# Masks first, a bf16 gate product of three exact parts, and the scores of two heads side by side

## Chip, cores and metric

The kernel runs on one core of one Trainium2 chip. The metric is the device time of one execution in microseconds (us), the median of the runs; lower is better.

## The reference

The program has three parts. Block 1 is two layers of a hybrid attention over 256 tokens of width 1024; block 2 is a gated delta-rule scan with a context of 256 rows; behind it stand 16 experts and a final norm. The change lies in block 1 alone. Each of its layers projects the modulated rows to 4032 columns and mixes three kinds of attention with heads of 64:

```python
def dsa_mixer(q, k, v, iq, ik, iw):      # 4 heads, one key head; block of 128 queries
    isc = einsum("bthd,bsd->bths", iqb, ik)
    isc = einsum("bth,bths->bts", iwb, relu(isc))
    _, idx = top_k(where(causal, isc, -inf), topk)      # topk = 64
    p = masked_softmax(einsum(qb, k[idx]) * scale, idx <= tpos)
...
def fox_mixer(q, k, v, logf):            # 6 heads
    cum = cumsum(logf, axis=1)
    s = einsum("bthd,bshd->bhts", qb, k) * scale
    s = s + cum[t] - cum[s]              # forget gates
    p = masked_softmax(s, causal)
...
def nsa_mixer(q, q_rot, kc, vc, ks, vs, kw, vw, gates):   # 6 heads, 2 groups of keys
    s = einsum("btgjd,bcgd->bgjtc", qb, kc) * scale       # 15 compressed keys
    p_cmp = masked_softmax(s, cend <= tpos)
    ...                                   # selected blocks and window: at 256 tokens both plain causal
    o = g0 * o_cmp + g1 * o_slc + g2 * o_win
```

With 256 tokens the selection and the window of the third kind take in everything that is causal, so each is an ordinary causal attention.

## The kernel before

A layer of block 1 (`layer`) goes through 17 chunks of projection columns. Each chunk's weights come by DMA into one of two tiles `w`, are split into two exact halves (`halves`, ScalarE and VectorE or GpSimd) and multiplied on TensorE in three products of one pass each (`proj_t`, L419 to L421; `proj_n`, L443). As soon as a chunk has given the queries and keys of two heads, their attention is called: `dsa` for two pairs, `fox` for three, and `nsa`, which after the compressed branch calls a pair for each of three head pairs and two branches. That makes 2 sparse, 3 gated and 6 plain pairs a layer, 22 in both. Other work is put in by hooks: products of modulation vectors (`gemv`, L358), and parts of the context for block 2. The order of the instructions on each engine is laid down by a scheduler when the program is built, from the dependencies and its own estimates, so that products of several stages stand between one another on TensorE.

`pair` treats two heads at once. Head 0 has rows 0 to 63 of `qT` and `kT`, head 1 rows 64 to 127. The scores of a head fill a half of a PSUM tile `s` [128, 2, 512]: the later block of 128 queries against 256 keys in columns 0 to 255, the earlier block against 128 keys in columns 256 to 383. For each block and head the score opens the sum (L526), the gate product over 12 f32 rows follows in gated pairs (L529), and the mask closes it: a bf16 product of a scaled identity `bigI` with the triangle `trib` (L532) or with the sparse mask of `topk` (L534). Then come the maxima on VectorE (L536, L537), four exponentials on ScalarE (L545), scaling by the reciprocal sums, transposes through a second tile `s` (L572 to L574), copies out of it, and the products with the values (L562, L565). There are two tiles `s`; the indexer's scores (L788) and other transposes use them too.

The gate's operands are prepared behind the first chunk (`after_na`): cumulated log gates from a product, `foxr` by VectorE (L759) and `foxc` by ScalarE (L761); `fox_rows` (GpSimd, L771) makes one head's 12 rows. `nsa` computes the compressed scores by 12 products with 64 rows and 16 columns and 12 masks (L870, L871).

Block 2 and the experts follow. The experts' weights are loaded into tiles `rw` by SP (L1766, L1808), which lie where tiles of block 2 lay and wait for these.

Of the kernel before, what the change touches and what calls it, by code (L numbers as in the profile page):

```python
# [11 lines left out]
BF = mybir.dt.bfloat16  # L12
AF = mybir.ActivationFunctionType
ALU = mybir.AluOpType
AX = mybir.AxisListType
PSUM = bass.MemoryType.PSUM

D = 1024
T = 256
# [9 lines left out]
# the tiles of block 2 from the lowest address up, those first that are needed longest: the weights of the experts  # L29
# take over from above  # L30
# [9 lines left out]
# ---------------------------------------------------------------- layout of the columns  # L40
# [65 lines left out]
# ---------------------------------------------------------------- constants of the shapes  # L106
def _consts():
    p = np.arange(128)
    c = {}
# [34 lines left out]
    # [cum8; -cum8] rows to the two operands of the forget-gate product  # L144
    fx = np.zeros((128, 14))
    for h in range(6):
        fx[h, h] = 1            # a1*hm
        fx[6 + h, 6 + h] = 1    # a0*hm
    fx[6:12, 12] = 1            # b1
    fx[0:6, 13] = 1             # b0  # L150
# [31 lines left out]
def prep(inp):  # L182
    """Layout of the inputs: transposes, slices, permutations of rows and columns."""
    f = {k: np.asarray(v) for k, v in inp.items()}
    a = {}
# [48 lines left out]
class Kern:  # L234
# [12 lines left out]
    def after(self, last):  # L247
        """what follows on the engine of this instruction is issued behind it"""
        return self.tc.issue_after(last.ins) if last is not None else nullcontext()
# [5 lines left out]
    def scope(self, name, psum=True, order=()):  # L255
        """pools for the working tiles of one part of the program"""
# [15 lines left out]
    def side(self):  # L272
        """what blocks 1 and 2 share: parts of the weights, and the rows of the context"""
# [7 lines left out]
    # ---- tiles  # L281
# [39 lines left out]
    # ---- exact halves of an operand: w = hi + lo, both of the type that goes through in one pass  # L321
# [21 lines left out]
    def gemv(self, w_dram, sec, vec, b_row, whole=False):  # L343
        """rows 32j.. of [128, 256]: columns 256j.. of the section of w_dram"""
# [19 lines left out]
    def cols(self, acc, outs):  # L364
        """outs: (i, out [128, 8], add, gain): out = (columns of the vector at row i + add) * gain"""
# [13 lines left out]
    def bcast(self, acc, out, add):  # L379
        """out [128, 1024]: the vector on every partition, plus add"""  # L380
# [25 lines left out]
    # ---- projections  # L406
# [6 lines left out]
    def proj_t(self, out, w, uT):  # L413
        """out [128 columns, 256 t]; w [128, 8, 128]"""
# [1493 lines left out]
```

## Time and profile before

| | |
|---|---|
| median of three runs | 1374.69 us (1373.82 to 1382.97) |
| the profiled execution, span from first to last instruction | 1373.8 us; it lies 0.9 us below the median |
| TensorE matmuls busy | 1122.8 us, 82% |
| VectorE busy | 566.2 us, 41% |
| ScalarE busy | 389.0 us, 28% |
| GpSimd busy | 274.7 us, 20% |
| HBM read | 327.51 MB, 239 GB/s over the span |
| mean granted TensorE clock | 0.872 |

A busy share is a mean over stages that have different limits; what counts is the share in the stage of the change. The duration of a matmul in the trace is that of its way through the array, and one begins before the one ahead has ended; so what an instruction takes from TensorE is read from its start to the next start. An f32 product appears as two instructions (x2).

### The profile page before, as it was taken

The numbers are of one execution on the slowest core, as the hardware profiler recorded it, in microseconds if no ns is written. First come the engines' busy times: TensorE is split into PE (matmuls) and PEld (weight loads), VectorE is DVE, ScalarE is ACT, GpSimd is POOL, SyncE is SP. The second block draws the span as 40 slices with busy tenths as digits, with TensorE's granted clock in tenths as the row PEclk, the third lists the DMA queues.
The fourth block names the chain that finished last, engine by engine and source line by source line (L and its number), as shares of the span: only waits on it lengthen the run. The fifth ranks groups of instructions, "written<-read, shape, count | busy, mean of one in ns | idle before, by whom it ended". The sixth has DMA issues, their size and how long they took to land.

```text
span 1373.8 us, 22174 instructions
## 1 busy us (share of the span) xinstructions
PE 1122.8 (82%) x9158; PEld 788.2 (57%) x9158; DVE 566.2 (41%) x1307; ACT 389.0 (28%) x891; POOL 274.7 (20%) x235
## 2 busy tenths in 40 slices
PE   5889999987879999993988989989766666676665
PEld 2667687676756877672977977765422232232222
DVE  2484235767587233559667545641100010010002
ACT  2242234745333332644444242520000000000001
POOL 1431031156420121125334434200000000000000
PEclk9998988998988798996997999999866787788876
DMA  9745854342415245660212153879999999999996
GB/s 336 266 152 174 308 189 146 102 159 102 161 62 170 92 171 186 233 203 14 93 36 81 62 215 125 340 277 408 411 409 411 410 410 411 408 412 409 411 412 231
DMA packets 93526, 330.01 MB, mean 240 GB/s; under 512 B 8048, under 2 KB 22256, under 8 KB 87024
## 3 DMA queue, kind: packets, MB, share of 16 engines
q1 hardware_dynamic: 93424, 328.58, 63.8%
q8 instruction: 72, 1.18, 0.3%
q14 instruction: 30, 0.25, 0.0%
HBM read 327.51 MB, written 1.05 MB: 239 GB/s over the span
## 4 chain that ended last, share of the span: by engine, by line
DMA 27%; PE 26%; DVE 4%; ACT 3%; issue 3%; POOL 2%; SPq 0%; POOLq 0%; DVEq 0%; ACTq 0%
DMA rw<-in_w_up 13%; DMA rw<-in_w_down 9%; DMA rw<-in_w_gate 5%; PE s L1281 3%; PE s L461 2%; PE mm L419 2%; PE mm L420 2%; PE mm L421 2%; PE g L1770 1%; PE mm L1813 1%; PE s L526 1%; PE mm L443 1%; PE s L1417 1%; PE o L1770 1%; PE g L358 1%
## 5 line engine op out<-in xcount | busy, mean ns | idle before, releaser
L421 PE MATMUL mm<-uT,wl 128*128 128x256 f32 x576 | 168.6, 295 | 17.4 <-DVE wl L331 9.1
L419 PE MATMUL mm<-uT,wh 128*128 128x256 f32 x576 | 173.9, 302 | 9.9 <-DVE yT L1216 6.1
L330 ACT CAST wh<-w 128x1024 fp32r<-128x1024 f32 x124 | 127.7, 1034 | 181.9 <-PE mm L420 112.0
L420 PE MATMUL mm<-uT,wh 128*128 128x256 f32 x576 | 169.0, 294 | 0.0
L331 POOL TENSOR_TENSOR wl<-w,wh 128x1024 fp32r<-128x1024 f32 x47 | 116.1, 2473 | 205.3 <-ACT wh L330 204.1
L421 PEld LDWEIGHTS mm<-uT,wl 128*128 128x128 f32 x576 | 112.8, 197 | 24.6 <-DVE wl L331 10.2
L419 PEld LDWEIGHTS mm<-uT,wh 128*128 128x128 f32 x576 | 113.9, 198 | 21.8 <-issue 8.8
L1770 PE MATMUL g<-rw,XE 128*32 128x256 f32 x928 | 86.9, 483 | 43.0 <-DMA rw<-in_w_up 43.0
L1770 PE MATMUL o<-rw,XE 128*32 128x256 f32 x944 | 89.0, 482 | 36.3 <-DMA rw<-in_w_gate 36.3
L420 PEld LDWEIGHTS mm<-uT,wh 128*128 128x128 f32 x576 | 113.8, 197 | 5.5 <-issue 4.9
L331 DVE TENSOR_TENSOR wl<-w,wh 128x1024 fp32r<-128x1024 f32 x77 | 96.7, 1256 | 46.8 <-ACT wh L330 46.5
L1786 DVE TENSOR_TENSOR hd<-hd,g 128x256 f32<-128x256 f32 x16 | 6.7, 419 | 219.0 <-PE g L1770 219.0
L1782 ACT ACTIVATE hd<-o 128x256 f32<-128x256 f32 x16 | 6.1, 384 | 320.6 <-PE o L1770 320.6
L1770 PEld LDWEIGHTS g<-rw,XE 128*32 128x32 f32 x928 | 32.1, 129 | 90.1 <-DMA rw<-in_w_up 70.7
L1813 PE MATMUL mm<-rw,hT 128*32 128x256 f32 x880 | 64.2, 426 | 23.9 <-DMA rw<-in_w_down 18.3
L1770 PEld LDWEIGHTS o<-rw,XE 128*32 128x32 f32 x944 | 31.8, 129 | 83.5 <-DMA rw<-in_w_gate 59.1
L443 PE MATMUL mm<-wh,uT 128*128 128x256 f32 x256 | 62.2, 330 | 3.2 <-ACT wh L330 2.5
L526 PE MATMUL s<-qk 64*128 64x256 f32 (+1 forms) x176 | 57.2, 408 | 0.3 <-DVE qk L514 0.2
L1813 PEld LDWEIGHTS mm<-rw,hT 128*32 128x32 f32 x880 | 27.3, 119 | 51.9 <-DMA rw<-in_w_down 27.0
L443 PEld LDWEIGHTS mm<-wh,uT 128*128 128x128 f32 x256 | 49.0, 228 | 7.4 <-ACT wh L330 2.9
L545 ACT ACTIVATE P<-s,nm 128x256 f32<-128x256 f32 (+1 forms) x88 | 35.8, 419 | 40.9 <-DVE nm L538 40.9
L443 PE MATMUL mm<-wl,uT 128*128 128x256 f32 x128 | 42.5, 332 | 0.7 <-DVE wl L331 0.7
(640 smaller groups left out, 2116.5 us busy)
## 6 DMA issues: line engine op xcount, KB each, us to landing
rw<-in_w_gate SPq DMA_DIRECT2D x59, 1024.0 KB, 18.4
rw<-in_w_up SPq DMA_DIRECT2D x58, 1024.0 KB, 18.4
rw<-in_w_down SPq DMA_DIRECT2D x55, 1024.0 KB, 18.6
w<-in_w_in SPq DMA_DIRECT2D x48, 1024.0 KB, 4.9
wg<-in_w_mod SPq DMA_DIRECT2D x24, 1024.0 KB, 5.2
wg<-in_w_ada SPq DMA_DIRECT2D x21, 1024.0 KB, 5.8
w<-in_w_out SPq DMA_DIRECT2D x12, 1024.0 KB, 4.9
w<-in_w_up SPq DMA_DIRECT2D x6, 1024.0 KB, 19.2
```

Of the source, the lines that this page charges most:

```text
L330: self.nc.scalar.copy(hi, w)
L331: self.lo_engine().tensor_sub(lo, w, hi)
L419: mm(out, wh[:, k, :], uh[:, k, :], start=(k == 0), stop=False)
L420: mm(out, wh[:, k, :], ul[:, k, :], start=False, stop=False)
L421: mm(out, wl[:, k, :], uh[:, k, :], start=False, stop=(k == 7))
L443: mm(p[:, tt, :], a[:, k, t], b[:, k % 4, :], start=(k == 0 and tt == 0 and j == 0), stop=(k == 7 and j == 2), skip_group_check=True)
L461: mm(Y(tt, n), a[:, t], b[:, 512 * n:512 * n + 512], start=(k2 == 0 and kk == 0 and i == 0), stop=(k2 == 3 and kk == 1 and i == 2))
L526: nc.tensor.matmul(S[:, h, o:o + n], qT[rows, 128 * tt:128 * tt + 128], kT[rows, :n], start=True, stop=False)
L545: nc.scalar.activation(Pm[:, h, o:o + n], S[:, h, o:o + n], AF.Exp, bias=nm[:, i:i + 1], scale=0.125, accum_out=l[:, i:i + 1])
L1281: self.nc.tensor.matmul(p[:, h, :], x[:, h, :], y[:, h, :], start=True, stop=True)
L1770: nc.tensor.matmul(pp[32 * j:32 * j + 32, :], XE[:, k, 32 * (e % 4):32 * (e % 4) + 32], w[:, kk, 256 * j:256 * j + 256], start=(k == 0), s ...
L1813: nc.tensor.matmul(py[32 * j:32 * j + 32, :], hT[:, cb, 32 * jj:32 * jj + 32], w[:, kk, 256 * j:256 * j + 256], start=(k == 0), stop=(k == 7))
```

## The change

In `pair`, all masks are now multiplied first and open the sums: for each head one product of `bigI` with the triangle twice side by side (columns 128 to 383), or with the whole sparse mask (columns 0 to 383), which is now one tile for both blocks of queries. Then come the gate products of both heads, and last the scores, block by block, head 0 and head 1 behind one another.

The gate product changes its form. The cumulated sums are made three times, on rows 0, 32 and 64, and split into three bf16 parts whose sum is the f32 value; `foxc`, `foxr` and `foxl` have 96 bf16 rows in place of 12 f32 ones.

In `nsa` the compressed keys of both groups stand in one [128, 32] tile, each in its own 16 columns, the rest zero. One product gives all masks, and six products over all 128 rows give the scores of a pair of heads at once.

```diff
     def pair(...):
         S = self.pst()
-        for tt in (1, 0):
-            n = 256 if tt else 128
-            o = 0 if tt else 256
+        for h in range(2):
+            if dsamask is None:
+                nc.tensor.matmul(S[:, h, 128:384], self.bigI, self.trib[:, None, :].to_broadcast([128, 2, 128]),
+                                 start=True, stop=False, skip_group_check=True)
+            else:
+                nc.tensor.matmul(S[:, h, 0:384], self.bigI, dsamask, start=True, stop=False, skip_group_check=True)
+        blocks = ((0, 256, slice(128, 256)), (256, 128, slice(0, 128)))
+        if fox is not None:
+            lh, rh = fox
             for h in range(2):
-                rows = slice(64 * h, 64 * h + 64)
-                nc.tensor.matmul(S[:, h, o:o + n], qT[rows, 128 * tt:128 * tt + 128], kT[rows, :n], start=True, stop=False)
-                if fox is not None:
-                    lh, rh = fox
-                    nc.tensor.matmul(S[:, h, o:o + n], lh[h][:12, 128 * tt:128 * tt + 128], rh[:12, :n],
-                                     start=False, stop=False)
-                if dsamask is None:
-                    nc.tensor.matmul(S[:, h, o + n - 128:o + n], self.bigI, self.trib, start=False, stop=True)
-                else:
-                    nc.tensor.matmul(S[:, h, o:o + n], self.bigI, dsamask[tt][:, :n], start=False, stop=True)
+                for o, n, t in blocks:
+                    nc.tensor.matmul(S[:, h, o:o + n], lh[h][:, t], rh[:, :n], start=False, stop=False,
+                                     skip_group_check=True)
+        for o, n, t in blocks:
+            for h, rows in enumerate(HALF):
+                nc.tensor.matmul(S[:, h, o:o + n], qT[rows, t], kT[rows, :n], start=False, stop=True,
+                                 skip_group_check=True)
...
     def after_na(self, N, bf, S):
-        lf = self.t([128, 2, 12], "lf")
+        lf = self.t([128, 2, 3, 32], "lf")
+        nc.gpsimd.memset(lf, 0.0)
...
-        cu = self.psg([12, 256])
+        cu = self.psg([96, 256])
...
-        S["foxr"] = self.t([12, 256], "foxr")
-        nc.vector.tensor_scalar(S["foxr"], cu, fx[:12, 12:13], fx[:12, 13:14], op0=ALU.mult, op1=ALU.add)
-        S["foxc"] = self.t([12, 256], "foxc")
-        nc.scalar.copy(S["foxc"], cu)
+        S["foxc"] = F = self.t([96, 256], "foxc", 1, BF)
+        nc.scalar.copy(F, cu)
+        r = self.t([96, 256], "foxd")
+        for j in (slice(32, 64), slice(64, 96)):
+            nc.vector.tensor_sub(r[j], cu[j], F[j])
+            nc.vector.tensor_copy(F[j], r[j])
+        j = slice(64, 96)
+        nc.vector.tensor_sub(r[j], r[j], F[j])
+        nc.vector.tensor_copy(F[j], r[j])
+        S["foxr"] = self.t([96, 256], "foxr", 1, BF)
+        nc.vector.tensor_scalar(S["foxr"], F, fx[:96, 12:13], fx[:96, 13:14], op0=ALU.mult, op1=ALU.add)
...
     def fox_rows(self, S, h):
-        a = self.t([12, 256], "foxl", 3)
+        a = self.t([96, 256], "foxl", 3, BF)
...
     def topk(self, S):
-        S["dmask"] = {}
+        S["dmask"] = mask = self.t([128, 384], "dmask", 1, BF)
...
-            mk = self.t([128, n], f"dmask{tt}", 1, BF)
+            mk = mask[:, o:o + n]
...
     def cmp_finish(self, cc, S):
-        S["kcT"] = self.t([128, 16], "kcT")
-        nc.scalar.copy(S["kcT"], p[:, 0:16])
+        S["kcT"] = self.t([128, 32], "kcT")
+        nc.gpsimd.memset(S["kcT"], 0.0)
+        for g, rows in enumerate(HALF):
+            nc.scalar.copy(S["kcT"][rows, 16 * g:16 * g + 16], p[rows, 0:16])
...
     def nsa(self, S):
-        ps = self.pst()
+        ps = self.pst()[:, 0, 0:192].rearrange("p (x g c) -> p x g c", g=2, c=16)
+        nc.tensor.matmul(ps.rearrange("p (a i) g c -> p a (i g) c", a=2), self.bigI,
+                         self.cmb[:, :, None, :].to_broadcast([128, 2, 6, 16]), start=True, stop=False, skip_group_check=True)
         for tt in range(2):
             for i in range(3):
-                for g in range(2):
-                    r = slice(64 * g, 64 * g + 64)
-                    o = ps[:, g, (tt * 3 + i) * 16:(tt * 3 + i) * 16 + 16]
-                    nc.tensor.matmul(o, S[f"nq{i}"][r, 128 * tt:128 * tt + 128], S["kcT"][r, :], start=True, stop=False)
-                    nc.tensor.matmul(o, self.bigI, self.cmb[:, tt, :], start=False, stop=True)
+                nc.tensor.matmul(ps[:, 3 * tt + i], S[f"nq{i}"][:, 128 * tt:128 * tt + 128], S["kcT"], start=False,
+                                 stop=True, skip_group_check=True)
```

`HALF` is the pair of slices (0 to 63, 64 to 127). The rest of the diff takes out comments.

## Rows read from the trace of the kernel before

**Rows 1.** Stages: us; PE, PEld, DVE, ACT, POOL busy; clock, DMA share, GB/s

```profile
100.00:300.00 200.00, 197.14 (x1375) 147.63 (x1368) 97.56 (x235) 85.96 (x219) 43.45 (x35) 0.92 0.52 181
300.00:404.00 104.00, 77.02 (x534) 69.15 (x532) 79.29 (x190) 45.82 (x99) 50.05 (x42) 0.87 0.33 112
404.00:617.00 213.00, 209.09 (x1450) 156.18 (x1449) 102.69 (x251) 81.37 (x214) 38.45 (x33) 0.90 0.51 173
...
925.00:1374.00 449.00, 308.84 (x3422) 139.75 (x3411) 40.58 (x119) 24.98 (x66) 0.00 (x0) 0.79 1.00 396
```

**Rows 2.** The DMA queue's waits: total us, times, longest

```profile
SPq L1766 <- PE s L1281: 15.8, 2, 8.1
```

**Rows 3.** Timeline of TensorE, a gated pair: start us, duration us, instructions

```profile
484.64 0.70 PE L526 MATMUL s<-qk 64*128 64x256 f32 x2
485.26 0.69 PE L529 MATMUL s<-foxr,foxl 12*128 12x256 f32 x2
485.89 0.23 PE L532 MATMUL s<-trib,bigI 128*128 128x128 bf16 x1
486.05 0.70 PE L526 MATMUL s<-qk 64*128 64x256 f32 x2
...
487.46 0.48 PE L526 MATMUL s<-qk 64*128 64x128 f32 x2
487.88 0.48 PE L529 MATMUL s<-foxr,foxl 12*128 12x128 f32 x2
...
489.32 0.43 PE L443 MATMUL mm<-wl,uT 128*128 128x256 f32 x1
```

**Rows 4.** Timeline of TensorE, projection and the indexer's scores

```profile
64.81 0.28 PE L421 MATMUL mm<-uT,wl 128*128 128x256 f32 x1
64.93 0.28 PE L419 MATMUL mm<-uT,wh 128*128 128x256 f32 x1
...
66.43 0.70 PE L788 MATMUL s<-qk 32*128 32x256 f32 x4
67.06 0.70 PE L510 MATMUL o<-rraw,c 128*128 128x256 f32 x2
...
70.69 0.71 PE L788 MATMUL s<-qk 32*128 32x128 f32 x8 [0.62 <-ACT irel L791]
71.34 0.39 PE L421 MATMUL mm<-uT,wl 128*128 128x256 f32 x1
```

**Rows 5.** Timeline, first sparse pair of the first layer

```profile
91.63 0.28 PE L534 MATMUL s<-dmask,bigI 128*128 128x256 bf16 x1
...
91.85 0.70 PE L526 MATMUL s<-qk 64*128 64x256 f32 x2
...
96.06 0.22 PE L534 MATMUL s<-dmask,bigI 128*128 128x128 bf16 x1
```

**Rows 6.** Timeline of TensorE, compressed scores of the first layer

```profile
207.21 0.61 PE L870 MATMUL s<-kcT,qk 64*128 64x16 f32 x2
...
207.88 0.61 PE L870 MATMUL s<-kcT,qk 64*128 64x16 f32 x2
```

**Rows 7.** Busy time where the granted clock is low, two of seven stretches

```profile
202.00:217.00 15.00, 15.00 (x69) 10.53 (x70) 4.04 (x11) 0.36 (x1) 1.45 (x1) 0.54 0.20 66
438.00:459.00 21.00, 21.00 (x82) 15.14 (x83) 4.03 (x13) 4.14 (x14) 3.10 (x3) 0.51 0.16 51
```

**Rows 8.** Line L759: count, ns min/median/max, first and last start us

```profile
L759 DVE TENSOR_SCALAR foxr<-g,c x2: 524/528/531, 49.1 to 360.7; 12x256 f32<-12x256 f32 x2
```

**Rows 9.** Timeline, a plain pair of the second layer

```profile
573.07 0.70 PE L526 MATMUL s<-qk 64*128 64x256 f32 x2
...
577.01 0.23 PE L532 MATMUL s<-trib,bigI 128*128 128x128 bf16 x1
...
582.19 0.33 PE L572 MATMUL s<-c,P 128*128 128x128 f32 x1
...
582.99 0.70 PE L526 MATMUL s<-qk 64*128 64x256 f32 x2
```

More of the change, by code (lines that the diff above doesn't have):

```diff
@@ L145, in _consts @@
     fx = np.zeros((128, 14))
[L146 to L150, printed above, removed]
+    for j in range(0, 96, 32):
+        for h in range(6):
+            fx[j + h, h] = 1
+            fx[j + 6 + h, 6 + h] = 1
+        fx[j + 6:j + 12, 12] = 1
+        fx[j:j + 6, 13] = 1
     c["fx"] = fx
@@ L749, in after_na @@
         nc.scalar.activation(e, e, AF.Ln, bias=1.0)
-        lf = self.t([128, 2, 12], "lf")
+        lf = self.t([128, 2, 3, 32], "lf")
+        nc.gpsimd.memset(lf, 0.0)
         nc.vector.tensor_scalar(x, x, 0.0, None, op0=ALU.min)
-        nc.vector.tensor_sub(lf[:, :, 0:6], x, e)
-        nc.vector.tensor_sub(lf[:, :, 6:12], e, x)
-        cu = self.psg([12, 256])
-        nc.tensor.matmul(cu, lf[:, 0, :], self.c["cumU"], start=True, stop=False)
-        nc.tensor.matmul(cu[:, 128:256], lf[:, 1, :], self.c["cumU"][:, 0:128], start=False, stop=True)
-        fx = self.c["fx"]
-        S["foxr"] = self.t([12, 256], "foxr")
-        nc.vector.tensor_scalar(S["foxr"], cu, fx[:12, 12:13], fx[:12, 13:14], op0=ALU.mult, op1=ALU.add)
-        S["foxc"] = self.t([12, 256], "foxc")
-        nc.scalar.copy(S["foxc"], cu)
+        three = lambda a: a[:, :, None, :].to_broadcast([128, 2, 3, 6])
+        nc.vector.tensor_sub(lf[:, :, :, 0:6], three(x), three(e))
+        nc.vector.tensor_sub(lf[:, :, :, 6:12], three(e), three(x))
+        cu = self.psg([96, 256])
+        lw = lf.rearrange("p a j r -> p a (j r)")
+        nc.tensor.matmul(cu, lw[:, 0, :], self.c["cumU"], start=True, stop=False)
+        nc.tensor.matmul(cu[:, 128:256], lw[:, 1, :], self.c["cumU"][:, 0:128], start=False, stop=True)
+        fx = self.c["fx"]
+        S["foxc"] = F = self.t([96, 256], "foxc", 1, BF)
[9 more added lines that the diff above has]
+        nc.vector.tensor_scalar(S["foxr"], F, fx[:96, 12:13], fx[:96, 13:14], op0=ALU.mult, op1=ALU.add)
         g = self.t([128, 2, 18], "ng")
@@ L767, in fox_rows @@
     def fox_rows(self, S, h):
-        a = self.t([12, 256], "foxl", 3)
+        a = self.t([96, 256], "foxl", 3, BF)
         fx = self.c["fx"]
-        self.nc.gpsimd.tensor_scalar(a, S["foxc"], fx[:12, h:h + 1], fx[:12, 6 + h:7 + h], op0=ALU.mult, op1=ALU.add)
+        self.nc.gpsimd.tensor_scalar(a, S["foxc"], fx[:96, h:h + 1], fx[:96, 6 + h:7 + h], op0=ALU.mult, op1=ALU.add)
         return a
@@ L820, in topk @@
                                            op0=ALU.is_gt, op1=ALU.max)
-            S["dmask"][tt] = mk
     def mix_out(self, S, j, O):
@@ L862, in nsa @@
         nc = self.nc
-        ps = self.pst()
+        ps = self.pst()[:, 0, 0:192].rearrange("p (x g c) -> p x g c", g=2, c=16)
+        nc.tensor.matmul(ps.rearrange("p (a i) g c -> p a (i g) c", a=2), self.bigI,
+                         self.cmb[:, :, None, :].to_broadcast([128, 2, 6, 16]), start=True, stop=False, skip_group_check=True)
         for tt in range(2):
             for i in range(3):
-                for g in range(2):
-                    r = slice(64 * g, 64 * g + 64)
-                    o = ps[:, g, (tt * 3 + i) * 16:(tt * 3 + i) * 16 + 16]
-                    nc.tensor.matmul(o, S[f"nq{i}"][r, 128 * tt:128 * tt + 128], S["kcT"][r, :], start=True, stop=False)
-                    nc.tensor.matmul(o, self.bigI, self.cmb[:, tt, :], start=False, stop=True)
+                nc.tensor.matmul(ps[:, 3 * tt + i], S[f"nq{i}"][:, 128 * tt:128 * tt + 128], S["kcT"], start=False,
+                                 stop=True, skip_group_check=True)
         sc = self.t([128, 2, 2, 3, 16], "csc")
-        nc.vector.tensor_scalar(sc.rearrange("p g a i c -> p g (a i c)"), ps[:, :, 0:96], 0.125, -2.0 ** 96,
-                                op0=ALU.mult, op1=ALU.max)
+        nc.vector.tensor_scalar(sc.rearrange("p g a i c -> p g (a i) c"), ps.rearrange("p x g c -> p g x c"), 0.125,
+                                -2.0 ** 96, op0=ALU.mult, op1=ALU.max)
         mx = self.t([128, 12], "cmx")
```

## The prediction

> **What bounds the kernel now.** I began with the busy times by stage [rows 1]. From 100 to 300 us (the first layer of block 1 from its attention on) and from 404 to 617 us (the same of the second layer) TensorE is busy 197 of 200 and 209 of 213 us, while VectorE and the DMA queues have about half of the time each. Between them, 300 to 404 us, TensorE has 77 of 104 and VectorE 79: no single engine bounds that. From 925 us on DMA has all of the time: the experts' weights stream in. So in the two attention stretches a microsecond less of TensorE work should be a microsecond, if nothing else steps in. Does it last to the end? The weight loads of the experts are issued by SP, and they wait for tiles that block 2 lets go: 15.8 us behind the transposes of L1281 in one group [rows 2]. The DMA-bound part therefore starts when block 2 gets there, and time gained in block 1 is passed on.
>
> Then I read what a pair of heads costs. In a pair with forget gates [rows 3] one head's score over 256 keys holds TensorE 0.62 us (from start to next start, 484.64 to 485.26), the gate product 0.63, the mask 0.16 (485.89 to 486.05); over 128 keys a score takes 0.42, and the gate product of the same columns as much. From the first score to the next stage it is 4.68 us. What of this is columns? A score is two passes (x2 in the row), and 128 columns more in both cost 0.62 - 0.42 = 0.20, so 0.10 to 0.11 for 128 columns in one pass; 0.20 us of each product is left over. In the projections, where all products have one shape, 256 columns follow each other by 0.12 us with nothing left over [rows 4]. In the pair, rows and shape change at every step (64, 12, 128 rows).
>
> **The change, part by part.** *Scores side by side.* Nothing of before shows 64-row products of two heads in succession, but the indexer's scores use rows in the same manner: four passes, two 32-row products over 256 keys, last 0.63 us (66.43 to 67.06) [rows 4], no more than one 64-row product; and eight passes over 128 keys, two row groups with two products behind each other, last 0.65 (70.69 to 71.34). So both heads over 256 keys should cost 0.63, and both over 128 keys, in the same row shape and with nothing to change over, 2 x 0.107 = 0.21 more: 0.84 us in place of 2 x (0.62 + 0.42) = 2.08. If they don't run beside each other: 4 x 0.21 + 4 x 0.107 + 0.20 = 1.48. I take 0.84, the nearer row.
>
> *Masks.* Four masks become two of 256 columns (384 in the pairs of the sparse attention). One of 256 takes 0.21 us, rounded from 91.63 to 91.85 [rows 5]; a second of the same shape adds its columns, 0.11. So 0.32 in place of 4 x 0.16 = 0.64, and 0.43 in place of 2 x 0.21 + 2 x 0.16 = 0.74. A mask that reads one block twice has no row; its bounds are 0.32 and 0.43.
>
> *Gate products.* Four f32 products of 2 x (0.63 + 0.42) = 2.10 us become four bf16 ones over 96 rows, one pass each. Bounds: columns alone, 2 x 0.11 + 2 x 0.07 = 0.35; a mask's price for each, 4 x 0.16 = 0.64. They stand behind masks of nearly the same shape, so I take 0.40.
>
> The Trainium skill ("TensorEngine Tiling (Array Packing)", Key Properties) says that a change of the tiling mode, not of the tile alone, drains TensorE; it knows modes of 32, 64 and 128 rows, so 96 rows behind 128 would drain nothing, and the six pairs would cost 6 x 0.05 = 0.3 us less than by my 0.40 and 1.7 less than by the 0.64. The 0.20 us left over in rows 3 agree with the rule; a product of 96 bf16 rows no row here shows.
>
> *Sum over pairs.* Plain pairs (12): 2.08 + 0.64 = 2.72 becomes 1.16, gain 1.56, together 18.7. Gated pairs (6): 4.68 becomes 1.56, gain 3.12, together 18.7. Sparse pairs (4): 2.82 becomes 1.27, gain 1.55, together 6.2.
>
> *Compressed scores.* Twelve scores and twelve masks a layer become one mask and six full-row products of 32 columns. A score with its mask takes 0.67 us where the clock is low (207.21 to 207.88) [rows 6]: 12 of them 8.0 us, and half of that if all ran at the full level. I take 7, since most of that stage is low [rows 7]. Then: twelve passes of at least 0.11 and a mask, 1.5, or twice that at the low clock; I take 2. Gain 5 a layer, 10 in all.
>
> Together 18.7 + 18.7 + 6.2 + 10 = 54 us of TensorE.
>
> *The clock.* From 100 to 300 us the granted clock is 0.92, from 404 to 617 us 0.90 [rows 1]; between its levels of 1.2 and 2.4 GHz that is 0.16 x 200 + 0.20 x 213 = 75 us at the lower one. It is down where the small products sit: 0.54 from 202 to 217 us (the compressed scores) and 0.51 from 438 to 459 us (behind the compression, in gated pairs) [rows 7]. With these products fewer and fuller, part of this should return. At most 75/2 = 37 us, of which I estimate 9 to be in the prices above already: 0 to 28. I take 15, a choice: the compression's own products, ahead of 438, aren't touched and may still bring the clock down.
>
> *What is added.* Behind the first projection, five VectorE passes over 32 rows, a memset and a multiply over 96 rows. The nearest row is the one that builds the gate rows from PSUM, 0.53 us for the same columns [rows 8]: at most 5 x 0.53 = 2.7 us a layer, more than 50 us ahead of the first gated pair, on an engine that is idle half of the time; 0 to 5.4 us in all. If that idle time is gone it delays the top-k on VectorE in a stretch that TensorE doesn't bound. I take 1. The gate rows by GpSimd keep their engine and number of columns; the copies of the compressed keys lie far ahead of their use. 0 each.
>
> *The order.* In the sparse pairs the mask now comes first and for both blocks of queries at once, so no score runs before the top-k ends. Before, scores and masks of the later block ran from 91.63 us while VectorE still sorted, and only the last masks waited until 96.06 [rows 5]. Behind that, one score and two masks remained, 0.42 + 2 x 0.16 = 0.75 us; now all 1.27. What waits behind it on TensorE are projections that would have to run later anyway. Loss 0.5 for the first sparse pair of a layer, and its gain of 1.55 falls in time that was idle: at most 2 a layer, 4 in all.
>
> *How much arrives.* 54 + 15 - 1 - 4 = 64 us of TensorE time. I let four fifths arrive, 52: in the stretches TensorE is busy 98% of the time and the others half, but each pair has a chain through other engines, and the order of TensorE's instructions is laid down when the program is built and will come out differently. Bounds are three fifths and all. The profiled execution lasts 1373.8 us, 0.9 below the median of the runs: 1373.8 - 52 + 0.9 = 1323 us, rounded.
>
> **Rivals.** (a) *The two heads don't overlap*, or the order separates them. For it: in the pair from 573.07 to 577.01 the scores and masks take 3.94 us instead of 2.72, since other products stand in between [rows 9]. Against it: the indexer rows. It takes 22 x 0.64 = 14 us from the 64; four fifths of 50 are 40: 1335.
>
> (b) *The chain of a pair sets the pace in the plain pairs.* From the first score to that of the next pair 9.92 us pass (573.07 to 582.99), of which the last mask to the transposes, through maxima, exponentials and scaling, takes 5.2 (577.01 to 582.19) [rows 9]. For it: that half isn't TensorE's and stays. Against it: the scores are in that chain too, so it shortens with them, and other products fill TensorE meanwhile. If half of the plain pairs' gain and the clock's 15 are lost: four fifths of 64 - 9 - 15 = 32: 1343.
>
> The Trainium skill ("TensorEngine Tiling (Array Packing)", PSUM Bottleneck) says that tiling speeds up TensorE and not the emptying of PSUM. That is this rival; the 5.2 us bear it out as part of the chain, not as its bound.
>
> (c) *Masks take the score tiles too early: slower.* There are two score tiles, shared by scores, transposes, indexer and context. A mask needs nothing but the tile, so it may be placed long before queries and keys exist; from then on the pair ahead has one tile in place of two. Price: the 5.2 us from scores to transposes [rows 9], in which no such work could start. It decides if TensorE then stands idle for more than 64/22 = 2.9 us a pair; with all 5.2, 22 x 5.2 - 64 = 50 us slower: 1425. Against it: projections fill TensorE in such gaps now.
>
> (d) *Nothing arrives*: loads or VectorE pace the stretches. The halves of rows 1 speak against it. 1374.
>
> **How the numbers follow.** Forecast 0.64, (a) 0.12, (b) 0.12, (d) 0.07, (c) 0.05. The range: low end, all of the pairs' 54 and all of the clock's 28: 1374.7 - 82 = 1293. High end, (a), a third of the clock and three fifths: 0.6 x (54 - 14 - 5 + 5) = 24, less 2 for the additions: 1353. That holds the forecast, (a) and (b), 0.88 less their own spread. A measurement of this kernel tells about 1%, 14 us, from no change: faster 0.87, within 1% 0.08, slower 0.05.
>
> **What would show it.** In the profile after: no f32 gate products, from first mask to last score of a gated pair about 1.6 us in place of 4.68; the two heads' scores in one row of 0.7 us; compressed scores done within 2 to 3 us; a granted clock of 0.95 or more in the two stretches; block 2 and the first experts' load some 50 us earlier, and the part behind them as long as before. It would be wrong if the heads stood 0.2 us or more apart (a); if a short score phase left a pair's period near 10 us (b); if transposes or projections waited for a score tile (c); if TensorE idled with SP or VectorE as releasers (d).

## The result and the profile after

The changed kernel takes 1327.25 us (median of 4 runs, 1324.58 to 1332.24) beside 1374.67 us of the kernel before in the same comparison: ratio 0.964, 95% interval 0.9604 to 0.9676. The forecast was 1323 with a range of 1293 to 1353. Run again with the last group of experiments it took 1324.98 us (5 runs) beside 1380.84, ratio 0.9595 (0.9568 to 0.9622). So the gain is 47 to 56 us; most of the difference between the two lies in the kernel before.

The busy times by stage of the changed kernel, cut at the same places of the program as [rows 1]; the columns are as there:

```profile
100.00:279.00 179.00, 171.71 (x1325) 131.52 (x1314) 102.44 (x235) 86.48 (x227) 43.06 (x36) 0.97 0.57 202
279.00:385.00 106.00, 78.51 (x542) 70.13 (x540) 81.76 (x196) 45.83 (x100) 49.75 (x43) 0.87 0.30 110
385.00:567.00 182.00, 175.26 (x1398) 133.35 (x1398) 104.75 (x250) 81.41 (x215) 38.89 (x33) 0.99 0.59 205
877.00:1325.00 448.00, 310.19 (x3422) 142.85 (x3414) 40.60 (x119) 24.95 (x66) 0.00 (x0) 0.79 1.00 397
```

The two attention stretches are 21 and 31 us shorter, the one between them and the DMA-bound end are as long as before. The first product of the experts starts at 868.3 us in place of 916.2, the last at 1314.3 in place of 1362.2: what block 1 gained is passed on to the end, one for one. The granted clock is 0.97 and 0.99 in place of 0.92 and 0.90. TensorE now stands idle 7.3 of 179 and 6.7 of 182 us, together 14.0; before it was 2.9 and 3.9. SP's waits for the transposes of block 2, which carried that argument, are still there (longest 10.5 in place of 8.1 us) [rows 2]:

```profile
SPq L1784 <- PE s L1299: 18.6, 2, 10.5
```

Timeline of TensorE in the changed kernel (start us, duration us, instructions), a gated pair:

```profile
448.95 0.39 PE L527 MATMUL s<-trib,bigI 128*128 128x256 bf16 x2
449.18 0.49 PE L536 MATMUL s<-foxr,foxl 96*128 96x256 bf16 x4
449.49 0.37 PE L445 MATMUL mm<-wl,uT 128*128 128x256 f32 x1
...
450.40 0.92 PE L540 MATMUL s<-qk 64*128 64x256 f32 x8
451.26 0.39 PE L445 MATMUL mm<-wl,uT 128*128 128x256 f32 x1
```

The same view, the first sparse pair, then the compressed scores, then from a plain pair to the next:

```profile
96.76 0.50 PE L530 MATMUL s<-dmask,bigI 128*128 128x384 bf16 x2
97.19 0.92 PE L540 MATMUL s<-qk 64*128 64x256 f32 x8
98.04 0.39 PE L422 MATMUL mm<-uT,wh 128*128 128x256 f32 x1
...
192.09 0.26 PE L884 MATMUL s<-cmb,bigI 128*128 128x192 bf16 x1
192.19 0.56 PE L888 MATMUL s<-kcT,qk 128*128 128x32 f32 x4
192.58 0.38 PE L527 MATMUL s<-trib,bigI 128*128 128x256 bf16 x2
...
194.07 0.97 PE L888 MATMUL s<-kcT,qk 128*128 128x32 f32 x8
194.98 0.49 PE L540 MATMUL s<-qk 64*128 64x128 f32 x4
...
500.32 0.38 PE L527 MATMUL s<-trib,bigI 128*128 128x256 bf16 x2
500.63 0.92 PE L540 MATMUL s<-qk 64*128 64x256 f32 x6
501.47 0.65 PE L569 MATMUL o<-PT,NC 128*64 128x256 f32 x2
502.05 0.48 PE L540 MATMUL s<-qk 64*128 64x128 f32 x2
...
509.31 0.33 PE L579 MATMUL s<-c,P 128*128 128x128 f32 x1
...
510.02 0.38 PE L527 MATMUL s<-trib,bigI 128*128 128x256 bf16 x2
510.34 0.70 PE L540 MATMUL s<-qk 64*128 64x256 f32 x2
```

From start to next start: both masks of a gated pair 0.23 us, its four gate products 0.31, all scores of both heads 0.86 (450.40 to 451.26) and 0.85 in the sparse pair. A gated pair takes 1.40 us in place of 4.68 [rows 3], without the projections between. The compressed scores and their mask take 0.10 + 0.39 + 0.91 = 1.40 us a layer. Where two scores of different heads adjoin, their starts lie 6 to 7 ns apart in the single records. But these two plain pairs still follow each other by 9.70 us (500.32 to 510.02), where it was 9.92 [rows 9]. Over four periods it is 38.7 us for 39.7 in the second layer, but 38.1 for 41.0 in the first.

### The profile page after: what moved, and what is told of

The parts are those of the page before. It is cut to its first block, busy times and chain, and to the rows that moved or that the text cites. A ratio compares the mean times of both kernels' runs of the same rounds, so it can differ in the third digit from the quotient of the medians.

```text
span 1325.1 us, 21973 instructions
## 1 busy us (share of the span) xinstructions
PE 1068.3 (81%) x9044; PEld 756.0 (57%) x9044; DVE 578.2 (44%) x1319; ACT 389.2 (29%) x893; POOL 274.0 (21%) x239
## 4 chain that ended last, share of the span: by engine, by line
PE 43%; DMA 26%; DVE 13%; ACT 5%; issue 3%; POOL 3%; SPq 0%; POOLq 0%; DVEq 0%; ACTq 0%
DMA rw<-in_w_up 15%; DMA rw<-in_w_down 7%; PE mm L421 4%; PE mm L423 3%; PE mm L422 3%; PE s L463 3%; PE s L1299 3%; PE g L360 3%; PE mm L445 2%; DMA rw<-in_w_gate 2%; PE mm L1831 2%; PE g L1788 2%; PE s L540 2%; DMA w<-in_w_up 2%; PE o L569 1%
## 5 line engine op out<-in xcount | busy, mean ns | idle before, releaser
L1831 PE MATMUL mm<-rw,hT 128*32 128x256 f32 x880 | 67.8, 448 | 21.3 <-DMA rw<-in_w_down 15.6
L445 PE MATMUL mm<-wh,uT 128*128 128x256 f32 x256 | 57.4, 310 | 3.1 <-ACT wh L332 2.5
L445 PEld LDWEIGHTS mm<-wh,uT 128*128 128x128 f32 x256 | 44.2, 206 | 7.5 <-issue 3.0
L463 PE MATMUL s<-wh,m 128*128 128x512 f32 x128 | 40.8, 397 | 0.0
```

The costliest lines, as they stand in the source:

```text
L445: mm(p[:, tt, :], a[:, k, t], b[:, k % 4, :], start=(k == 0 and tt == 0 and j == 0), stop=(k == 7 and j == 2), skip_group_check=True)
L463: mm(Y(tt, n), a[:, t], b[:, 512 * n:512 * n + 512], start=(k2 == 0 and kk == 0 and i == 0), stop=(k2 == 3 and kk == 1 and i == 2))
L1831: nc.tensor.matmul(py[32 * j:32 * j + 32, :], hT[:, cb, 32 * jj:32 * jj + 32], w[:, kk, 256 * j:256 * j + 256], start=(k == 0), stop=(k == 7))
```

## Experiments

Times are medians. Three groups of kernels ran, each beside the kernel before on its chip (1381.01, 1378.61 and 1380.84 us); the ratio to that is what is compared.

| kernel | us (runs) | ratio, 95% interval |
|---|---|---|
| gate product alone | 1362.07 (6) | 0.9849 (0.9820 to 0.9879) |
| compressed scores alone | 1361.23 (4) | 0.9853 (0.9831 to 0.9875) |
| masks first and scores side by side alone | 1333.59 (4) | 0.9646 (0.9623 to 0.9668) |
| head by head | 1329.65 (6) | 0.9612 (0.9585 to 0.9640) |
| more TensorE work | 1348.97 (5) | 0.9786 (0.9756 to 0.9815) |
| longer chain | 1336.76 (5) | 0.9695 (0.9667 to 0.9722) |
| masks last | 1313.06 (6) | 0.9532 (0.9504 to 0.9560) |
| low halves on VectorE | 1315.70 (5) | 0.9540 (0.9511 to 0.9570) |
| the changed kernel again | 1324.98 (5) | 0.9595 (0.9568 to 0.9622) |
| masks last and low halves on VectorE | 1313.11 (5) | 0.9508 (0.9482 to 0.9535) |
| kernel before, low halves on VectorE | 1379.14 (12) | 0.9990 (0.9968 to 1.0012) |
| masks last in the plain pairs | 1314.81 (5) | 0.9526 (0.9503 to 0.9549) |

"Slots" below are the times from start to next start on TensorE, summed over the lines that the change edits: 93.9 us in the kernel before, 38.0 after. They are as long as the clock made them, so a slot also shrinks when the clock rises.

**The gate product alone, on the kernel before.** The three bf16 parts on 96 rows; scores and masks stay as they were.

```diff
-                    nc.tensor.matmul(S[:, h, o:o + n], lh[h][:12, 128 * tt:128 * tt + 128], rh[:12, :n],
+                    nc.tensor.matmul(S[:, h, o:o + n], lh[h][:, 128 * tt:128 * tt + 128], rh[:, :n],
...
-        S["foxc"] = self.t([12, 256], "foxc")
-        nc.scalar.copy(S["foxc"], cu)
+        S["foxc"] = F = self.t([96, 256], "foxc", 1, BF)
+        nc.scalar.copy(F, cu)
+        r = self.t([96, 256], "foxd")
...
```

> The kernel before with the gate product alone changed to 96 bf16 rows in one pass; order, masks and compressed scores as before. Theory 1 (TensorE's time in the two attention stretches arrives nearly whole at the end): in each of six gated pairs 2.10 us of f32 gate products become four single passes between other shapes, some 0.65 us, so 6 x 1.45 = 9 us of TensorE, and with a part of the low clock behind them returning 1360 to 1367 us. Rival (the chain of a pair through the other engines sets the pace): the gate product stands in that chain too, but most gated pairs lie among projections; 1370 to 1376 us.

Measured: about 20 us faster, for 17 us of slots, 12.9 of them the gate product's own. The window of [rows 7] at 438 us, which lay at 0.51, in this kernel:

```profile
438.00:459.00 21.00, 20.80 (x151) 15.98 (x151) 9.86 (x29) 8.53 (x25) 3.50 (x3) 1.00 0.31 101
```

The clock stands at its upper level there and the window holds 151 instructions in place of 82. The part brings more than its own slots.

**The compressed scores alone, on the kernel before.**

```diff
-                    nc.tensor.matmul(o, S[f"nq{i}"][r, 128 * tt:128 * tt + 128], S["kcT"][r, :], start=True, stop=False)
-                    nc.tensor.matmul(o, self.bigI, self.cmb[:, tt, :], start=False, stop=True)
+                nc.tensor.matmul(ps[:, 3 * tt + i], S[f"nq{i}"][:, 128 * tt:128 * tt + 128], S["kcT"], start=False,
+                                 stop=True, skip_group_check=True)
```

> The kernel before with the compressed scores alone changed (one mask, six full-row products a layer). Theory 1: 7 us a layer become 1.5 to 2, and the low clock from 202 to 217 and from 523 to 537 us shortens: 10 to 16 us in all, so 1358 to 1365 us. Rival (chain sets the pace in the plain pairs behind it): the compressed scores stand ahead of the first plain pair's values, not ahead of its scores, so they would have been hidden: 1371 to 1376 us.

Measured: about 20 us faster, for 16 us of slots, 11.2 of them the compressed scores' and their masks' own. Here the other stretch of [rows 7] is gone; where it stood at 0.54, this kernel's compressed scores run at the upper level:

```profile
196.00:212.00 16.00, 16.00 (x150) 11.90 (x149) 9.60 (x33) 5.94 (x17) 4.34 (x6) 1.00 0.76 270
```

**Masks first and scores side by side alone, on the kernel before.** The gate product stays f32 on 12 rows, the compressed scores stay as they were.

```diff
+        for h in range(2):
+            if dsamask is None:
+                nc.tensor.matmul(S[:, h, 128:384], self.bigI, self.trib[:, None, :].to_broadcast([128, 2, 128]),
+                                 start=True, stop=False, skip_group_check=True)
...
+                    nc.tensor.matmul(S[:, h, o:o + n], lh[h][:12, t], rh[:12, :n], start=False, stop=False,
+                                     skip_group_check=True)
+        for o, n, t in blocks:
+            for h, rows in enumerate(HALF):
+                nc.tensor.matmul(S[:, h, o:o + n], qT[rows, t], kT[rows, :n], start=False, stop=True,
+                                 skip_group_check=True)
```

> The kernel before with the order of the pair alone changed: masks first, then the f32 gate products of 12 rows together, then both heads' scores side by side; compressed scores as before. Theory 1: plain pairs 12 x 1.56, sparse 4 x 1.55 less 4, gated 6 x (1.56 + 0.6) us, 34 us of TensorE, of which four fifths arrive: 1344 to 1352 us. Rival (chain): the plain pairs in the changed kernel still follow each other by some 9.7 us, so their 18.7 us are lost and 12 to 16 arrive: 1358 to 1364 us.

Measured: about 49 us faster, for 38 us of slots. That is nearly the whole change. The parts don't add up: 20 + 20 + 49 = 89 us alone, 47 to 56 together. Part of the reason is the clock. In the attention of both layers, from the first score to the end of the output product, it lies at its lower level for 71.8 us in the kernel before, 41.0 with the gate product alone, 51.2 with the compressed scores alone, 17.1 with this part alone, 13.7 (6.8 in the second profile) with all three. Half of what goes is 15, 10 and 27 us, 53 in sum, but 29 (32) with all three. This part takes back nearly all of it, so the other two, which earned more than their own slots when they stood alone, find little left.

**Head by head, on the changed kernel.** First both blocks of head 0, then both of head 1, so that the program no longer names scores of the two heads in turn for each block.

```diff
-        for o, n, t in blocks:
-            for h, rows in enumerate(HALF):
+        for h, rows in enumerate(HALF):
+            for o, n, t in blocks:
```

> The changed kernel with the scores of one head over both blocks first and then those of the other, so that the long products of the heads are no longer next to each other; nothing else differs, and the row shape changes as rarely as in the changed kernel. If overlap of the heads is what the order of the scores gives: 0.64 us a pair less what the last of the first head and the first of the second still share, 0.43 x 22 = 9.5 us of TensorE, 1332 to 1338 us. If it's the rarer change of shape alone: 1325 to 1330 us, and the two heads' passes stand one behind the other in both kernels.

Measured: 0.9612, between the two results of the changed kernel. The slots of the scores grow from 26.2 to 29.4 us, 3.2, in place of the 14 that rival (a) put on the loss of the overlap. So the order in the program hardly decides whether they overlap: in seven pairs all scores of both heads still stand next to each other. What the overlap is worth shows in this kernel's timeline where other products stand between the heads:

```profile
118.98 0.92 PE L540 MATMUL s<-qk 64*128 64x256 f32 x4
119.82 0.43 PE L569 MATMUL o<-PT,NA 128*64 128x256 f32 x1
...
120.62 0.92 PE L540 MATMUL s<-qk 64*128 64x256 f32 x4
121.46 0.39 PE L445 MATMUL mm<-wl,uT 128*128 128x256 f32 x1
```

One head alone takes 0.84 us (118.98 to 119.82, and 120.62 to 121.46), as much as both side by side, 0.85. Where they adjoin, the second head is all but free.

**More TensorE work, on the changed kernel.** Two further rounds of eight products of low halves in the chunks of the output gates, estimated at 29 us in sum (32.7 by their slots); they add a term of the size of the rounding to the gates.

```diff
+        for n in range(more):
+            for k in range(8):
+                mm(out, wl[:, k, :], ul[:, k, :], start=False, stop=(k == 7 and n == more - 1))
...
+                self.proj_t(q, w[:, :, 128 * ti:128 * ti + 128], uT, 2 if name[0] == "g" else 0)
```

> The changed kernel with 16 more one-pass products of 256 columns in each of the eight gate tiles of a layer (the product of the two low halves, added twice, so the gates differ by a rounding): 8 x 16 x 0.113 = 14.5 us of TensorE a layer, 29 us in all, in the stretch of the plain pairs and outside their chain. If TensorE still paces that stretch, 25 to 29 us arrive: 1352 to 1357 us. If the plain pairs' chain through the other engines paces it since the change, the idle time of TensorE takes a part: at most 15 arrive, 1328 to 1342 us.

Measured: 0.9786, which is 20 us more than 0.964 and 26 more than 0.9595. Of 29 (32.7) us 20 to 26 arrive: TensorE still paces most of the stretches, but not all. In the second layer the plain pairs follow each other faster here than in the changed kernel, though their masks come first too and TensorE has more to do; the masks of two in succession on TensorE:

```profile
524.34 0.38 PE L530 MATMUL s<-trib,bigI 128*128 128x256 bf16 x2
...
532.97 0.38 PE L530 MATMUL s<-trib,bigI 128*128 128x256 bf16 x2
```

The period is 8.6 us (8.6 to 8.9 from the second plain pair on) in place of 9.70. So 9.70 is the length that one order gives, not a floor that the pair's chain sets.

**A longer chain, on the changed kernel.** The maxima of VectorE twice in the plain pairs, 13.2 us in sum, no work for TensorE.

```diff
+        if gates is not None:
+            nc.vector.tensor_reduce(nm[:, 0:2], S[:, :, 0:256], axis=AX.X, op=ALU.max)
+            nc.vector.tensor_reduce(nm[:, 2:4], S[:, :, 256:384], axis=AX.X, op=ALU.max)
```

> The changed kernel with the two maxima of each plain pair taken twice: 1.1 us more on VectorE in the chain of each of twelve pairs, 13.2 us in all, and nothing more on TensorE. If TensorE paces the plain pairs: 0 to 4 us slower, 1327 to 1331 us. If the chain paces them: 10 to 13 us slower, 1337 to 1341 us.

Measured: 0.9695, 8 us more than 0.964, 14 more than 0.9595. Over half of it arrives, although VectorE is busy half of the time: the chain of a pair, rival (b), does have a hold on the plain pairs. In the profile the attention of both layers has 19.2 us of idle TensorE in place of 14.0 (12.9 in the second profile) and 27.3 us at the lower clock in place of 13.7 (6.8), so more of the loss comes by the clock than by the idle time itself.

**Masks last, on the changed kernel.** Scores open the sum, then the gate products, then the masks.

```diff
+        for o, n, t in blocks:
+            for h, rows in enumerate(HALF):
+                nc.tensor.matmul(S[:, h, o:o + n], qT[rows, t], kT[rows, :n], start=(o == 0), stop=False,
+                                 skip_group_check=True)
...
+                nc.tensor.matmul(S[:, h, 128:384], self.bigI, self.trib[:, None, :].to_broadcast([128, 2, 128]),
+                                 start=False, stop=True, skip_group_check=True)
```

> The changed kernel with the order within a pair turned round: both heads' scores side by side first, then the gate products, then the two wide masks. The same products and as many changes of shape. If it's the products and their shapes that count, the same time within 4 us, 1323 to 1331 us; in the gated pairs mask and gate products no longer run ahead of the queries and keys (0.6 us each, 4 us in all), in the sparse pairs the scores no longer wait for the top-k (2 to 4 us back). If masks first held score tiles to the harm of others: 5 us or more faster, under 1322 us.

Measured: 0.9532, faster than the changed kernel in either of its results. In this kernel, putting the masks first costs.

**Low halves on VectorE, on the changed kernel.** From chunk 11 to the output product GpSimd gets none of the subtractions that split the weights.

```diff
-            self.pat = "P" if l == 0 and 3 <= i < 6 else "VVP"
+            self.pat = "P" if l == 0 and 3 <= i < 6 else "V" if i >= 11 else "VVP"
...
+        self.pat = "VVP"
```

> The changed kernel with the low halves of the weights from the third keys on (from chunk 11 to the output product) all on VectorE and none on GpSimd. In the profile of the changed kernel two of VectorE's 0.35 us scalings in the second layer's plain pairs last 2.45 us, each until a GpSimd subtraction that runs beside it has ended, and TensorE stands still 1.5 to 1.7 us behind each. If such meetings lengthen the plain pairs: 3 to 6 us faster, 1321 to 1324 us, and plain pairs 8.7 us apart in the second layer. If not, or if the 1.25 us each on VectorE cost as much: 1326 to 1330 us.

Measured: 0.9540. What made me try it stands in the changed kernel at 518 us. The timeline of VectorE there, two scalings of the probabilities:

```profile
517.80 2.75 DVE L563 TENSOR_SCALAR P<-P,rl 128x256 f32<-128x256 f32 x2
```

The timeline of GpSimd, subtractions of the weights' halves:

```profile
518.04 2.35 POOL L333 TENSOR_TENSOR wl<-w,wh 128x1024 fp32r<-128x1024 f32 x1 [4.72 <-ACT wh L332]
537.34 2.36 POOL L333 TENSOR_TENSOR wl<-w,wh 128x1024 fp32r<-128x1024 f32 x1 [16.94 <-ACT wh L332]
```

And that of TensorE, a transpose that waited for the scaling (1.52 us idle before it):

```profile
520.60 0.33 PE L580 MATMUL s<-c,P 128*128 128x128 f32 x1 [1.52 <-DVE P L563]
```

Line L563 as a whole (ns min/median/max) in the changed kernel:

```profile
L563 DVE TENSOR_SCALAR P<-P,rl x44: 333/349/2481, 101.6 to 537.4; 128x256 f32<-128x256 f32 x44
```

The same line in the kernel with the low halves on VectorE:

```profile
L563 DVE TENSOR_SCALAR P<-P,rl x44: 340/348/827, 101.0 to 528.8; 128x256 f32<-128x256 f32 x44
```

Two scalings of 0.35 us take 2.75 together; the second ends at 520.55, 0.16 behind GpSimd's subtraction. The same happens at 537 us, and at both places of the second profile; a scaling at 132 us takes 2.18 us in the first profile alone. The Trainium skill ("SBUF — State Buffer", "SBUF: two separate sides") says that VectorE and GpSimd share a pair of ports, and that where a VectorE instruction needs it (a two-port mode, or two inputs from SBUF), whichever starts first holds the pair for its whole instruction and the other waits. The trace of the changed kernel agrees: a scaling ends just behind GpSimd's subtraction where that had started ahead of it, and keeps its 0.35 us where the subtraction started behind it, as here (two scalings, and a subtraction that starts 0.11 us behind the second):

```profile
101.59 0.62 DVE L563 TENSOR_SCALAR P<-P,rl 128x256 f32<-128x256 f32 x2
101.97 2.45 POOL L333 TENSOR_TENSOR wl<-w,wh 128x1024 fp32r<-128x1024 f32 x1 [12.44 <-ACT g_alog L1130]
```

**The changed kernel again.**

> The changed kernel itself, for the same chip and hour as the other runs of this group. Both theories: 1327 us, within 4 us, ratio 0.964 to the kernel before, within 0.004. It is the mark against which the differences below are taken.

Measured: 0.9595. The span of its profile is 1317.8 us, 7.3 less than that of the first, for the same program. One window of 10 us in the first profile:

```profile
125.00:135.00 10.00, 10.00 (x48) 7.80 (x46) 5.17 (x12) 4.01 (x14) 2.56 (x3) 0.51 0.37 117
```

And in the second:

```profile
125.00:135.00 10.00, 10.00 (x81) 6.85 (x83) 4.23 (x14) 4.61 (x16) 2.57 (x3) 1.00 0.54 159
```

Some low stretches come and go between executions of one program. A few microseconds between two profiles, or between two kernels, can be this alone.

**Both: masks last and low halves on VectorE.** The masks stand as in masks last; of the other edit it has the first line alone, and GpSimd gets as many subtractions of halves as with both lines (35).

```diff
...
-            self.pat = "P" if l == 0 and 3 <= i < 6 else "VVP"
+            self.pat = "P" if l == 0 and 3 <= i < 6 else "V" if i >= 11 else "VVP"
```

> The changed kernel with the masks last (alone 1313) and with all low halves of the plain chunks on VectorE (alone 1316). Theory 1, two causes: the masks' place and GpSimd's subtractions delay different instructions, so the gains of 14 and 12 us add up: 1297 to 1304 us. Theory 2, one cause: each of them only shifts the order of TensorE's queue so that the same waits and the same low-clock stretches (10 us at 125 us of the changed kernel) are gone, so the second finds little left: 1308 to 1315 us. What lies in between is a share of each.

Measured: 0.9508, 1313 us; with the masks last alone it was 1313 too. The gains don't add up: most of what one of them brings, the other has already brought (second theory).

**Low halves on VectorE, on the kernel before.** The same edit of `self.pat`.

> The kernel before, with all low halves of the plain chunks on VectorE and nothing else changed. Theory 1, the meetings of VectorE's scaling with GpSimd's subtraction are a cost that the change brought (the scaling of 0.35 us took 2.4 us beside one at 518 and 537 us of the changed kernel; in the kernel before no such meeting cost over 0.8 us): the kernel before gains under 4 us, 1371 to 1377. Theory 2, GpSimd is the wrong engine for them in either kernel: it gains the 12 us that the changed kernel gained, 1360 to 1366.

Measured: 0.9990 (0.9968 to 1.0012). Against its own chip's 1380.84 us that is 1.7 us, within the interval: no cost of GpSimd's subtractions is seen before the change. In the kernel before no such scaling lasts over 0.83 us; the long meetings came with the new order of the work (first theory). They don't belong to masks that come first: with masks first and scores side by side alone none lasts over 0.83 us either.

**Masks last in the plain pairs.** Gated and sparse pairs keep them first.

```diff
+        late = dsamask is None and fox is None
...
+        if not late:
+            masks(True, False)
...
+        if late:
+            masks(False, True)
```

> The changed kernel with the masks last in the plain pairs alone (6 of 11 in a layer); the gated and the masked pairs keep them first. Theory 1, masks that come first cost in the plain pairs, whose two triangles wait in TensorE's queue for a score tile that the pair before still holds: most of the 14 us of masks last is here, 1313 to 1318 us. Theory 2, they cost where the mask has a load of its own ahead of the scores (gated and masked pairs): 1322 to 1328 us. Theory 3, the 14 us are the order of the queue and the clock, and no place owns them: the time falls anywhere between 1310 and 1335 and bears no relation to the share of the pairs.

Measured: 0.9526. That is 10 us less than the changed kernel on the same chip, the same as with all masks last. The time fits the first theory, but the third as well. The first theory's mechanism, a score tile held early, isn't what the trace shows: in the changed kernel the masks start only 0.31 us ahead of the scores (500.32 to 500.63), right behind the transposes. Nor do all plain pairs gain: in the first layer the stretch from the first plain pair's scores to the last output product takes 81.3 us here, and 83.4 and 81.6 in the two profiles of the changed kernel. Most of the gain is in the second layer.

The stretch that decides is the last six pairs of the second layer up to the end of its output product. Busy times of it by windows, with columns as in [rows 1], in the kernel before:

```profile
523.00:620.00 97.00, 96.39 (x637) 70.47 (x641) 51.13 (x114) 42.63 (x117) 15.73 (x16) 0.93 0.59 203
```

In the changed kernel:

```profile
479.20:570.10 90.90, 87.31 (x638) 64.03 (x640) 53.80 (x114) 43.98 (x119) 18.11 (x17) 0.98 0.64 226
```

In the changed kernel again:

```profile
471.60:563.80 92.20, 88.61 (x637) 64.76 (x640) 53.78 (x114) 43.89 (x119) 18.38 (x17) 0.96 0.64 223
```

With masks first and scores side by side alone:

```profile
490.30:574.50 84.20, 83.59 (x595) 62.31 (x595) 47.60 (x112) 42.71 (x117) 15.00 (x14) 0.96 0.64 222
```

With masks last in the plain pairs:

```profile
473.50:557.70 84.20, 83.08 (x617) 61.70 (x620) 52.49 (x114) 43.26 (x119) 17.36 (x16) 1.00 0.66 232
```

With the low halves on VectorE:

```profile
471.90:560.10 88.20, 88.06 (x637) 64.36 (x640) 52.04 (x122) 43.22 (x119) 3.99 (x9) 0.96 0.67 233
```

The vector products (L360) alone in this stretch, the changed kernel again and masks last in the plain pairs (PE busy, PEld busy):

```profile
471.60:563.80 92.20, 11.80 (x164) 4.59 (x168) 0.96 0.64 223
473.50:557.70 84.20, 9.68 (x142) 3.80 (x146) 1.00 0.66 232
```

The change takes 6.1 us out of this stretch (4.8 in the second profile), though its scores, masks and compressed scores lose 11.6 us of slots there (22.4 to 10.9). TensorE's idle time grows from 0.6 to 3.6 us; the vector products take 1.6 us more from start to next start, since the order puts 164 of them here in place of 134; the products with the values take 1.4 more, half of it at the lower clock. With the masks last in the plain pairs the stretch lasts 84.2 us, 8.0 less than in the second profile of the changed kernel: idle 1.1, 22 fewer vector products (9.4 us in place of 11.3), and no 6.8 us at the lower clock. Without GpSimd's subtractions TensorE has no idle left here (88.06 of 88.20), and the stretch lasts 88.2. Masks first and scores side by side alone also come to 84.2, though with 32 vector products fewer and the compressed scores ahead of it. So the stretch differs by what the order puts into it, by idle time and by the clock; masks that come first don't lengthen it by themselves.

## Why the prediction was right

**What bounds it.** Right: two attention stretches that TensorE paces, a DMA-bound end that follows block 2. Added TensorE work arrives to 20 to 26 of 29 us.

**TensorE's 54 us.** Right in size: 56 us of slots. Scores of both heads 0.85 to 0.86 for the forecast 0.84; gate products 0.31 for 0.40; two masks 0.23 for 0.32, the sparse ones 0.43 for 0.43; compressed scores 1.40 a layer for 2. Either side of the difference is larger than my sums, 93.9 us for 86 before (12 x 2.72 + 6 x 4.68 + 4 x 2.82 + 14) and 38.0 for 32.4 after, since other products stand within the pairs and some ran at the lower clock; that the two errors nearly cancel is luck. The edited lines spent 32.8 of their 93.9 us at the lower clock, so 16 of the 56 us are the clock's, where I had put 9 into the prices: at the upper level the change takes out 40 us and not 45. The four gate products take 0.31 us behind the masks: the Trainium skill's rule ("TensorEngine Tiling (Array Packing)", Key Properties) that a change of mode drains TensorE, with 96 rows counted to the mode of 128, fits that better than my 0.40.

**The clock's 15 us.** Right in size. Of the 71.8 us at the lower level in the attention, 39.0 fell on lines that the change doesn't touch; after it is 13.7. Half of the difference, since one level is twice the other, is 12.7 us (16.4 in the second profile). The doubt about the compression's own products was answered by the parts: the stretch at 438 us is gone with the gate product alone, and with masks first and scores side by side alone too, which leaves the gate product in f32; the compressed scores alone leave it. So the compression's products don't hold the clock down by themselves.

**The additions and the order of the sparse pairs.** Not separable: 1 and 4 us lie within the scatter of the runs. The added VectorE passes are six and not five; they take 2.1 us a layer, under the 2.7 that I allowed, and end 65 us ahead of the first gated pair. For the 4 us there is no sign: masks last in the plain pairs alone and in all pairs come to the same time.

**Four fifths arrive.** Right in size: 56 + 13 = 69 us of TensorE, 47 to 56 measured, so 0.7 to 0.8. Where the rest went is shown for one place, the plain pairs of the second layer: 11.6 us of slots in, 6.1 out. From 60 us to the end of the second layer TensorE's work falls by 56 us and not by 69 (by 65 in the second profile), and its idle time grows by 6 us (40.6 to 46.9; by 9 in the second profile). What keeps the work from falling by all of the 69 is spread over small steps between products of several stages, and I can't put it in one place.

**Rivals.** (a) fell as to the overlap: adjoining heads start 6 to 7 ns apart, and both take what one takes alone. Its second half, that the order separates them, is there: in 15 of 22 pairs other products stand between heads or blocks, in 9 of these between the two heads, as at 510.34, and the scores have 26.2 us of slots in place of 22 x 0.84 = 18.5. (b) came true in part: in the second layer a plain pair's period is 9.70 us for 9.92, as its mark said, and added chain work arrives by more than half; but the period was 8.6 with more TensorE work. (c) is right that masks first cost in this kernel, 9 to 10 us, and most of it in the plain pairs of the second layer; but with masks first and scores side by side alone that stretch is as short as with the masks last, no score tile is seen held early, and the price was far too small to turn the sign. (d) fell.

What stays open: that masks last gain by a better order is read off the trace; why the scheduler arrives at it was not tested. Every edit gives all engines a new order, and no run holds the order fixed, so a difference of some 10 us between two kernels, that of the longer chain too, may be the order's and not the edit's own. Nor was a meeting of VectorE and GpSimd measured by itself, apart from the order that brings it.

## What to carry to other kernels

Sum a TensorE edit from start to next start, add the low-clock time of the work around it, and let it arrive only as far as the chain through the other engines permits: here 0.7 to 0.8. Parts that each free the same clock don't add up; try them singly and together. After such a change look again at choices that cost nothing before it, such as which engine does an elementwise step and what opens a PSUM sum: here two of them were worth 8 and 9 us against the changed kernel's second result, but together only 12. The best kernels here are those with the masks last, 1313 to 1315 us.

## What the runs showed of the hardware

- A scaling on VectorE (SBUF to SBUF, 128x256 f32) of 0.35 us lasted 2.48 us where a subtraction of 2.35 us on GpSimd had started just ahead of it, and ended 0.16 us behind it. Where the subtraction had started 1.8 us earlier, it lasted 0.76; where the subtraction started behind it, 0.35.
- f32 products of 64 rows on the two halves of the rows start 6 to 7 ns apart. The scores of one head (over 256 and over 128 keys) take 0.84 us alone, those of both heads side by side 0.85.
- bf16 products of 96 rows behind bf16 masks of 128 rows: 0.08 us a product (0.31 for two of 256 and two of 128 columns), nothing left over for the change of rows.
- One program, two executions: the window from 125 to 135 us at 0.51 of the full clock in one and at 1.00 in the other; the spans differ by 7.3 us.
